# Turned weights in four buffers, half a projection between them, and a first gate and up that are scaled by 1/rms afterwards

## The chip, the cores and the metric

The kernel runs on one core of a Trainium2 chip. The metric is the device time of one execution in microseconds (us). Before the change it was 3081.7 us, the median of 3 runs (3077.83 to 3083.58). TensorE is called PE here, VectorE DVE, ScalarE ACT, GpSimd POOL and SyncE SP.

## The reference

Two layers run over two groups of tokens that share all weights: a sample of 512 tokens and a prompt of 1024. The model width is 1024, the hidden width of the channel mixer 2816.

```python
def fourier_mixer(x, g, w):
    b, s, d = x.shape
    h = rms_norm(x, g).astype(jnp.float32).reshape(b, s, N_FGROUPS, FGROUP_DIM)
    mixed = jnp.real(jnp.fft.fft2(h, axes=(1, 3), norm="ortho"))
    return mixed.reshape(b, s, d).astype(x.dtype) @ w

def swiglu_ffn(x, g, w_gate, w_up, w_down):
    h = rms_norm(x, g)
    return (jax.nn.silu(h @ w_gate) * (h @ w_up)) @ w_down

for i in range(DEPTH):          # DEPTH = 2
    x = x + (fourier_mixer(...) if i % 2 == 0 else attention_mixer(...))
    x = x + swiglu_ffn(x, norm_ffn[i], ffn_w_gate[i], ffn_w_up[i], ffn_w_down[i])
```

The change concerns layer 0 of the sample: the Fourier mixer with its projection by `w`, and the norm, gate and up of the channel mixer behind it. Since 1/rms is one number for each token, it can be multiplied in before the gate's product or behind it.

## The kernel before

**Blocks and precision.** The tokens are three blocks of 512: block 0 is the sample, blocks 1 and 2 are the prompt. Activations stand turned, 128 features on the partitions and 512 tokens along the row. Each operand of a product is kept as a high and a low half, and `mm3` (lines 247 to 249) makes three matmuls of it: high by high, high by low, low by high. `split` (240, 241) makes the halves: ACT copies the high one, DVE or, if asked, POOL subtracts for the low one. `weights` loads a 512 KB chunk on SP, ACT casts it (278) and POOL subtracts (279).

**Order.** A planner orders each engine's queue: an instruction may be put ahead of others that stand earlier in the program, when its inputs and buffers are ready by the planner's model. `pinned` forbids that for one instruction. On the chip each queue runs in the order so made. `tl` hands out tiles by tag; a tag has a fixed number of buffers (`BUFS`, line 150), and a new tile waits until the last use of the tile that held its buffer. `weave` (1122) advances a main generator and an auxiliary one by the numbers that they yield, so that the smaller share of its cost goes next. Tags that end in F are the main generator's, those in X the auxiliary one's.

**The sample's mixing.** The constants and rows are loaded, then `busy(56)` issues 56 dummy matmuls (258 to 262). `lead` (1173) weaves two things. `mixer` (428) squares and folds the rows (`prepared`, 396 to 412), scales and combines them (`unit`, 454), multiplies them along the tokens (`along`, 525) and handles the feature 64 of each group apart (`ends_folded`, 491; `stacked`, 607). `turned_weights` (613) builds the weights of the projection: `operand(n)` adds and subtracts the two halves of chunk n (631 on DVE, 632 on POOL), casts (634, ACT) and subtracts (635, POOL); `product(n)` multiplies it by the small Fourier matrix (9 matmuls), splits the result for the sample's own projection (`split` at 653) and writes a copy to memory (`cwd`) for the prompt. The operands `wm` have the four buffers of `acc` for the whole stage, with the sample's Fourier matrix and first combined rows in two of them. Two operands are made ahead of the first product. Raw chunks have two buffers (`rawX`), the sums `f` two (`rawF`).

**The sample's projection and first norm.** `follow` (1185) runs when all eight products are traced. `mixer_projection` (674) makes for each of 8 output chunks 25 matmuls, adds the residual on DVE (717 to 722), squares on ACT and adds up (333). The last chunk has `busy(10)` in it and `rstd_cols` (295) `busy(12)`. 1/rms is worked out by `rsqrt` (282) on DVE, spread over the partitions by `in_rows` (305), and `normed` (338) multiplies each chunk by it and splits it into the tile h, the low halves on POOL.

**The FFN of block 0** (`ffn`, 743) goes through 22 hidden chunks: gate and up, 24 matmuls each, silu on ACT (784), the product on DVE (785), the split into `mid`, and 8 down products of 3 matmuls, which run among the next chunk's gate and up and are added up on DVE (755). The first gate and up alternate. The gate's and up's results have one bank each (`gF`, two banks). Meanwhile the auxiliary generator `aux_0` (1198) loads the prompt's rows, mixes and projects them. Its first step, the loading, is taken before `follow`.

Of the kernel before, what the change touches and what calls it, by code (L numbers as in the profile page):

```python
# [17 lines left out]
P = 128  # L18
# [41 lines left out]
def dft_constants():  # L60
# [38 lines left out]
    for par in range(2):  # L99
        odd[64 * par + 1 : 64 * par + 64 : 2, [8 + 4 * par, 40 + 4 * par, 72 + 4 * par]] = 1.0  # L100
    alt = np.zeros((P, 4, 2, 64))
    for g in range(NC):
        alt[[g, 64 + g], g % 4, g // 4] = (-1.0) ** i
# [21 lines left out]
def trunk_kernel(ctx: ExitStack, tc: tile.TileContext, t: dict):  # L125
# [125 lines left out]
    early, resting = [], []  # L251
# [43 lines left out]
    def rstd_cols(y, sq, n):  # L295
# [4 lines left out]
        if first and not resting:  # L300
            resting.append(True)
            busy(12)
# [35 lines left out]
    def normed(b, gain, got, ab, held=None):  # L338
# [5 lines left out]
        if b in resident:  # L344
            for dc in range(NC):
                x = tmp()
                dve.scalar_tensor_tensor(x, resident[b][dc], gain[:, dc : dc + 1], r, op0=ALU.mult, op1=ALU.mult)
                split(h[:, 0, dc], h[:, 1, dc], x, eng=pool)
            got["h"] = h
            return  # L350
# [34 lines left out]
    def load_rows(seq):  # L385
# [6 lines left out]
        for c, x in enumerate(xs):  # L392
            (sp if c % 2 == 0 else act).dma_start(x, t[f"rows_{seq}"][:, c, :])
        whole[seq] = xs

    def prepared(seq, n, ga, gb, sums):
# [4 lines left out]
        for c, x in enumerate(whole[seq]):  # L401
# [8 lines left out]
            yield 1.0  # L410
# [17 lines left out]
    def mixer(seq, done, u, xrs, zz):  # L428
# [53 lines left out]
        def ends(c):  # L482

            return sums[c][:, 1].rearrange("p (j r a) -> p r j a", j=4, r=2)[:, :, :, 0]

        def groups(ap):
            return ap.rearrange("p (r j) -> p r j", r=2)

        z, zs = zz

        def ends_folded():
            for c in range(2):
                f = [col(8) for _ in range(2 * npair)]
                for i in range(npair):
                    ca, cb = 4 * i + c, 4 * i + 2 + c
                    dve.tensor_scalar(groups(f[2 * i]), ends(ca), r[:, ca : ca + 1], None, op0=ALU.mult)
                    if two:
                        dve.scalar_tensor_tensor(groups(f[2 * i + 1]), ends(cb), scal(cb)[0], groups(f[2 * i]), op0=ALU.mult, op1=ALU.add)
                for k in range(3):
                    at = slice(32 * k, 32 * k + 8)  # L500
                    if two:
                        dve.tensor_tensor(z[:, 2 * c, at], f[1], f[3], op=ALU.add)
                        dve.tensor_tensor(z[:, 2 * c + 1, at], f[1], f[3], op=ALU.subtract)
                    else:
                        dve.scalar_tensor_tensor(groups(z[:, c, at]), ends(c + 2), scal(c + 2)[0], groups(f[0]), op0=ALU.mult, op1=ALU.add)
# [854 lines left out]
```

## Time and profile before

| | |
|---|---|
| median of 3 runs | 3081.7 us (3077.83 to 3083.58) |
| the profiled execution | 3077.77 us, of which the span of instructions 3076.0 |
| PE busy in the span | 2985.8 us (97%) |
| DVE busy | 1642.7 us (53%) |
| ACT busy | 1219.5 us (40%) |
| POOL busy | 1279.8 us (42%) |
| mean granted clock of PE | 0.993 |

A row of a timeline has the start, the duration, the engine, the line, the operation, the tile written and those read, their shapes and how many such instructions are merged; in brackets the time that the engine stood idle before it, and what ended that. A row of groups has behind the count the busy time in us, the mean of one instruction in ns, and the idle time before them. A row of windows has the stretch and its length, then for each engine the busy time and the number of instructions, then the clock that PE was granted, as a share of the full one, the share of time in which the DMA engines were busy, and GB/s. PE's busy time counts dummy matmuls and those at a low clock in full, so a busy PE isn't always a useful one.

### The profile page before, as it was taken

To read this page: it belongs to the slowest core of one execution; us is meant where nothing else is said; L and a number is where in the kernel's file an instruction comes from. 1 tells how busy PE (TensorE), PEld (TensorE's weight loads), DVE (VectorE), ACT (ScalarE), POOL (GpSimd) and SP (SyncE) were. 2 spreads that over 40 slices of the span, in tenths; PEclk is the share of its full clock that TensorE was granted. 3 is DMA by queue.
4 is the path that set the end of the run, shared out by engine and by line. 5 is a ranking of instruction groups with operands and counts; after the bars stand their busy time and mean duration, and the time that the engine had idled before them with its cause. 6 is when DMAs were issued, how large, how long until landed. Compare 5 with 4: busy or idle time off the path is not lost.

```text
span 3076.0 us, 36978 instructions
## 1 busy us (share of the span) xinstructions
PE 2985.8 (97%) x14268; PEld 2448.0 (80%) x14268; DVE 1642.7 (53%) x2863; ACT 1219.5 (40%) x1749; POOL 1279.8 (42%) x583
## 2 busy tenths in 40 slices
PE   7999999999999999999999999999999999999999
PEld 5778888888877878888878788888787787877777
DVE  6775554634455543533464465665236555655556
ACT  4433332333466532333344577777324222222221
POOL 4434444443333454444433321222637644544452
PEclk8999999999999999999999999999999999999999
DMA  6435443332323544433343211212636411111111
GB/s 211 140 101 160 153 126 96 117 113 81 103 83 103 185 155 139 143 110 103 93 147 103 91 60 60 66 50 78 221 118 198 164 62 45 45 56 56 47 48 62
DMA packets 132080, 330.06 MB, mean 107 GB/s; under 512 B 14176, under 2 KB 28512, under 8 KB 131264
## 3 DMA queue, kind: packets, MB, share of 16 engines
q1 hardware_dynamic: 130112, 316.61, 32.0%
q0 software_dynamic: 928, 7.94, 0.7%
q10 hardware_dynamic: 864, 3.15, 0.3%
q8 instruction: 112, 1.84, 0.2%
q14 instruction: 64, 0.52, 0.1%
HBM read 280.45 MB, written 47.19 MB: 107 GB/s over the span
## 4 chain that ended last, share of the span: by engine, by line
PE 83%; POOL 5%; DVE 4%; DMA 3%; issue 3%; ACT 2%; SPq 0%; POOLq 0%; ACTq 0%; DVEq 0%
PE c L247 12%; PE c L248 12%; PE c L249 12%; PE g L249 10%; PE g L247 10%; PE g L248 10%; PE a L247 4%; PE a L249 4%; PE a L248 4%; PE c L1095 2%; POOL w L279 2%; POOL w L241 1%; DVE col L1078 1%; POOL h L241 1%; PE c L1028 1%
## 5 line engine op out<-in xcount | busy, mean ns | idle before, releaser
L279 POOL TENSOR_TENSOR w<-raw,w 128x1024 fp32r<-128x1024 f32 x354 | 846.1, 2400 | 1316.3 <-ACT w L278 1249.6
L755 DVE TENSOR_TENSOR acc<-c,acc 128x512 f32<-128x512 f32 x704 | 483.1, 689 | 473.5 <-PE c L249 469.8
L278 ACT CAST w<-raw 128x1024 fp32r<-128x1024 f32 x354 | 370.8, 1049 | 530.7 <-PE c L249 281.3
L247 PE MATMUL g<-h,w 128*128 128x512 f32 x1408 | 557.0, 396 | 4.8 <-ACT t L784 4.8
L248 PE MATMUL g<-h,w 128*128 128x512 f32 x1408 | 553.4, 393 | 0.6 <-POOL h L241 0.6
L249 PE MATMUL g<-h,w 128*128 128x512 f32 x1408 | 552.7, 393 | 0.0
L247 PE MATMUL c<-mid,w 128*128 128x512 f32 x1056 | 416.7, 397 | 11.6 <-DVE acc L755 9.1
L248 PE MATMUL c<-mid,w 128*128 128x512 f32 x1056 | 414.0, 392 | 2.2 <-DVE mid L241 2.2
L249 PE MATMUL c<-mid,w 128*128 128x512 f32 x1056 | 413.6, 392 | 0.0
L241 POOL TENSOR_TENSOR w<-raw,w 128x1024 fp32r<-128x1024 f32 (+1 forms) x101 | 228.3, 2268 | 337.5 <-ACT w L240 316.4
L865 DVE TENSOR_TENSOR acc<-c,acc 128x512 f32<-128x512 f32 x352 | 240.8, 689 | 191.3 <-PE c L249 190.6
L247 PEld LDWEIGHTS g<-h,w 128*128 128x128 f32 x1408 | 265.8, 189 | 59.5 <-ACT t L784 6.5
L249 PEld LDWEIGHTS g<-h,w 128*128 128x128 f32 x1408 | 266.0, 189 | 55.0 <-POOL w L279 0.3
L248 PEld LDWEIGHTS g<-h,w 128*128 128x128 f32 x1408 | 265.8, 189 | 53.4 <-POOL h L241 1.3
L247 PEld LDWEIGHTS c<-mid,w 128*128 128x128 f32 x1056 | 197.8, 188 | 73.7 <-DVE acc L755 20.3
L248 PEld LDWEIGHTS c<-mid,w 128*128 128x128 f32 x1056 | 198.5, 188 | 41.7 <-DVE mid L241 3.9
L249 PEld LDWEIGHTS c<-mid,w 128*128 128x128 f32 x1056 | 198.5, 188 | 40.5
L248 PE MATMUL c<-h,w 128*128 128x512 f32 x480 | 188.2, 392 | 3.2 <-POOL h L241 3.1
L247 PE MATMUL c<-h,w 128*128 128x512 f32 x480 | 189.1, 395 | 0.8 <-ACT h L240 0.8
L249 PE MATMUL c<-h,w 128*128 128x512 f32 x480 | 187.0, 390 | 0.0
L240 ACT CAST w<-raw 128x1024 fp32r<-128x1024 f32 (+1 forms) x101 | 100.3, 1000 | 202.6 <-PE a L249 86.6
L1077 DVE TENSOR_REDUCE col<-a 128x1 f32<-128x1024 f32 (+1 forms) x96 | 100.4, 1046 | 128.2 <-PE a L249 128.0
(349 smaller groups left out, 4775.6 us busy)
## 6 DMA issues: line engine op xcount, KB each, us to landing
raw<-in_down_dram SPq DMA_DIRECT2D x110, 512.0 KB, 3.6
raw<-in_gate_dram SPq DMA_DIRECT2D x88, 512.0 KB, 3.6
raw<-in_up_dram SPq DMA_DIRECT2D x88, 512.0 KB, 3.7
raw<-in_qkv_dram SPq DMA_DIRECT2D x36, 512.0 KB, 3.9
t<-xres SPq DMA_DIRECT2D x56, 256.0 KB, 3.9
raw<-in_wo_dram SPq DMA_DIRECT2D x24, 512.0 KB, 3.9
raw<-in_gate_dram SPq DMA_DIRECT2D x44, 256.0 KB, 2.7
raw<-in_up_dram SPq DMA_DIRECT2D x44, 256.0 KB, 3.1
```

What stands on the lines that cost most here:

```text
L240: act.copy(hi, src)
L241: eng.tensor_tensor(lo, src, hi.bitcast(F32), op=ALU.subtract)
L247: pe.matmul(out, lh, rh, start=first, stop=False)
L248: pe.matmul(out, lh, rl, start=False, stop=False)
L249: pe.matmul(out, ll, rh, start=False, stop=last)
L278: pinned(act.copy(flat[:, 0], raw)) if early else act.copy(flat[:, 0], raw)
L279: pool.tensor_tensor(flat[:, 1], raw, flat[:, 0].bitcast(F32), op=ALU.subtract)
L755: dve.tensor_tensor(acc[dc], ps, acc[dc], op=ALU.add)
L865: dve.tensor_tensor(acc, ps, acc, op=ALU.add)
L1028: pe.matmul(c[:, i : i + 1], sq[:, i * P : (i + 1) * P], ones[:, 0:1], start=True, stop=True)
L1077: dve.tensor_reduce(st[:, 0:1], s_in, op=ALU.max, axis=AX.X)
L1095: pe.transpose(tr[:, i * P : (i + 1) * P], p[:, kc * P : (kc + 1) * P], ident)
```

## The change

- `busy(56)` becomes `busy(36)`; the 10 and the 12 dummy matmuls around the projection's end go.
- The operands `wm` get four buffers of their own in the slot hB; the sample's mixed rows and constants move to hA. Three operands are made ahead of the first product. In the mixer the second pair of units comes ahead of the multiplications along the tokens, and more is yielded, so that products stand at other places.
- Four products are traced within `lead`, and the other four one by one between the first four steps of the projection.
- The table for feature 64 (`stage`) takes a buffer of `rawF` and is loaded behind the first two chunks. The groups of features have another order, so that the small reads and writes of `ends_folded` have fewer instructions; the first multiplication of each goes to ACT.
- Each projection step splits its residual times the gain straight into h, the low halves on DVE. `normed` isn't called for block 0. 1/rms is copied into `first["r"]`, and `ffn` multiplies gate and up of block 0 by it, for all 22 hidden chunks.
- The prompt's rows are loaded later, all on SP, within the weave of the FFN of block 0, which runs 10 steps alone first.

```diff
-        if first and not resting:
-            resting.append(True)
-            busy(12)
...
-            (sp if c % 2 == 0 else act).dma_start(x, t[f"rows_{seq}"][:, c, :])
+            (act if seq == "s" and c % 2 else sp).dma_start(x, t[f"rows_{seq}"][:, c, :])
...
-            yield 1.0
+            yield 4.0
...
-                    dve.tensor_scalar(groups(f[2 * i]), ends(ca), r[:, ca : ca + 1], None, op0=ALU.mult)
+                    act.activation(f[2 * i], ends(ca), AF.Copy, scale=r[:, ca : ca + 1])
...
-            yield 1.0
+            yield 5.0
         r64 = mpt.tile([P, 516], F32R, tag="r64", name=f"r64_{seq}")
         second = []
+        for c in range(2):
+            second.append(unit(1, c))
+            yield 5.0
         if two:
             ends_folded()
-            for c in range(2):
-                second.append(unit(1, c))
-                yield 1.0
...
-            if j < 2 and not two:
-                second.append(unit(1, j))
...
-            w = acc_tile("wm", [2, 2, TB], F32R)
+            w = moving_w[n % 4]
...
-        operand(0)
-        yield
-        operand(1)
-        yield
+        for n in range(3):
+            operand(n)
+            yield
         for n in range(NC):
             product(n)
-            if n + 2 < NC:
-                operand(n + 2)
+            if n + 3 < NC:
+                operand(n + 3)
             yield
...
             resident[0] = accumulators()
+            first["h"] = h_tile("B")
...
-                if not two and n == NC - 1:
-                    busy(10)
...
+                if not two:
+                    split(first["h"][:, 0, n], first["h"][:, 1, n], x, gain=g_ffn[0][:, n : n + 1])
                 new_residual(b, n, x, stays=not two)
...
+            if here:
+                dve.tensor_tensor(ga, ga, first["r"], op=ALU.mult)
+                dve.tensor_tensor(up, up, first["r"], op=ALU.mult)
             act.activation(s, ga, AF.Silu)
...
-    stage = h_slot("stage", F32, "A")[:, 0:D]
-    sp.dma_start(stage[0:96], t["wf64"])
+    stage = tl("raw", [D], F32, "rawF")
+    slot_a = h_slot("wm", F32R, "B")[:, 0 : 16 * TB].rearrange("p (s h k n) -> p s h k n", s=4, h=2, k=2)
+    moving_w = [slot_a[:, i] for i in range(4)]
...
-    busy(56)
+    busy(36)
...
         next(ws)
-        stacked(w64[0:96], stage[0:96], 64)
+        sp.dma_start(stage[0:96], t["wf64"])
         m = mixer("s", got_s, u_s, xrs_s, zz_s)
         for k, v in enumerate(m):
             yield v
-            if k in (1, 3) or k >= 5:
-                next(ws, None)
+            if k == 4:
+                stacked(w64[0:96], stage[0:96], 64)
+            if k in (1, 3, 6) or k in (8, 10, 12, 14):
+                next(ws)
+
+    def follow():
+        m = mixer_projection("s", got_s)
+        for k in range(4):
+            next(m)
+            next(ws)
+            yield 1.0
         for _ in ws:
             yield 1.0
-
-    def follow():
-        yield from mixer_projection("s", got_s)
+        yield from m
         next(early[2])
         early.clear()
-        yield from normed(0, g_ffn[0], first, "B")
+        first["r"] = tl("ss", [TB], F32, "ssF")
+        act.copy(first["r"], in_rows(rstd[0]))
...
     weave(lead(), 1.0)
-    cur[0] = "X"
-    for _ in range(1):
-        next(x_0)
     weave(follow(), 1.0)
-    weave(ffn(0, 0, lambda: first["h"]), FFN_US, x_0, (45.0 + 60.0) * SLACK)
+    weave(ffn(0, 0, lambda: first["h"]), FFN_US, x_0, (80.0 + 60.0) * SLACK, 10)
```

More of the change, by code (lines that the diff above doesn't have):

```diff
@@ L249, in mm3 @@
         pe.matmul(out, ll, rh, start=False, stop=last)
-    early, resting = [], []
+    early = []
     nxt, first = {}, {}
@@ L651, in product @@
                     for b in range(2):
-                        pe.matmul(od[0:96], odd[:, 8 - j : 104 - j], w[:, b, 0], start=j == 0 and b == 0, stop=j == 3 and b == 1)
+                        pe.matmul(od[0:96], odd[:, 8 - 2 * j : 104 - 2 * j], w[:, b, 0], start=j == 0 and b == 0, stop=j == 3 and b == 1)
                 split(wt[:, 0, k], wt[:, 1, k], ps)
@@ L699, in mixer_projection @@
             for i, b in enumerate(blocks):
-                if (i if two else n % 2) == 0:
+                if two and i:
+                    e, o = sides()
+                elif not two and n > 3 and n % 2:
+                    e, o = (tl("c", [TB], F32, "cX", pools["psX"]) for _ in range(2))
+                else:
                     e, o = bank(), bank()
-                else:
-                    e, o = sides()
                 c0 = 258 * i
```

46 lines of the change are left out of this document (19 added, 27 removed).

## Prediction

> **What bounds the kernel now.** I read the page's busy rows first, then a table of windows cut at the stages of the sample block, then the timeline of those stages.
>
> ```profile
> span 3076.0 us, 36978 instructions
> ...
> PE   7999999999999999999999999999999999999999
> ```
>
> TensorE (PE) is busy 97% of the span. Only the first of 40 slices, 77 us each, is below nine tenths. Whatever this change wins by keeping PE fed it can win only there and in the thin places just behind.
>
> ```profile
> core 0: us, PE busy (x) PEld busy (x) DVE busy (x) ACT busy (x) POOL busy (x), PEclk, DMA share, GB/s
> 22.70:84.30 61.60, 41.21 (x145) 28.41 (x143) 42.68 (x81) 30.15 (x55) 27.89 (x16) 0.78 0.60 197
> 84.30:108.40 24.10, 24.10 (x201) 23.98 (x200) 16.59 (x47) 7.86 (x14) 3.77 (x4) 1.00 0.40 141
> 108.40:118.90 10.50, 9.59 (x78) 9.01 (x77) 5.14 (x20) 6.24 (x14) 6.71 (x4) 1.00 0.50 157
> 118.90:131.10 12.20, 11.53 (x48) 8.75 (x48) 9.86 (x16) 10.56 (x20) 10.08 (x8) 1.00 0.10 39
> 131.10:141.90 10.80, 7.36 (x24) 5.57 (x24) 10.80 (x19) 6.19 (x10) 4.76 (x2) 0.84 0.39 123
> 160.00:280.00 120.00, 111.19 (x589) 92.19 (x588) 77.53 (x163) 45.99 (x75) 48.79 (x21) 0.99 0.39 126
> 280.00:540.00 260.00, 260.00 (x1276) 220.27 (x1275) 133.22 (x249) 75.20 (x97) 112.36 (x47) 1.00 0.41 128
> ```
>
> The columns are busy times and instruction counts. From 22.7 to 84.3 the weights are turned and the sample is mixed. From 84.3 to 108.4 comes its projection, 201 matmuls in 24.1 us, 0.12 us each: dense, at clock 1.00. From 108.4 to 118.9 lies the normalization, then the first gate and up (48 matmuls) to 131.1, and the change to the second gate. From 280 on PE has no idle time, with DVE busy 133 of 260 us.
>
> ```profile
> 483.94 0.39 PE L247 MATMUL c<-mid,w 128*128 128x512 f32 x1
> ...
> 484.62 0.39 PE L247 MATMUL g<-h,w 128*128 128x512 f32 x1
> ```
>
> Three 512-wide matmuls in a stream take 0.68 us, 0.227 each. So the 48 of the first gate and up need 10.9 us of their 12.2, and the 24 records behind them 5.4 of 10.8 us.
>
> In 22.7 to 84.3 the code issues eight products of 9 matmuls (72 x 0.227 = 16.3 us) and 69 mixing matmuls of 0.12 (8.3): 24.6 us of work in 61.6. The other 37 us are waits and a clock of 0.78. Who makes PE wait there?
>
> ```profile
> L635 POOL TENSOR_TENSOR wm<-f,wm 128x1024 fp32r<-128x1024 f32 x8 | 18.9, 2369 | 24.1 <-ACT wm L634 24.1
> ...
> L632 POOL TENSOR_TENSOR f<-raw 128x512 f32<-128x512 f32 x8 | 11.3, 1413 | 19.6 <-DMA raw<-in_wf_dram 19.4
> ...
> L241 DVE TENSOR_TENSOR w<-g,w 128x512 fp32r<-128x512 f32 x16 | 10.9, 687 | 10.7 <-ACT w L240 10.7
> ...
> L631 DVE TENSOR_TENSOR f<-raw 128x512 f32<-128x512 f32 x8 | 8.0, 1006 | 0.0
> ```
>
> One operand costs POOL 1.41 + 2.37 = 3.8 us, eight 30 us. POOL is busy 27.9 of the 61.6 us, so it isn't full either; POOL itself stands still 24.1 us for ACT's cast and 19.6 for a load.
>
> ```profile
> 31.19 1.26 POOL L632 TENSOR_TENSOR f<-raw 128x512 f32<-128x512 f32 x1 [6.20 <-DMA raw<-in_wf_dram]
> ...
> 58.29 2.37 POOL L635 TENSOR_TENSOR wm<-f,wm 128x1024 fp32r<-128x1024 f32 x1 [5.38 <-ACT wm L634]
> ```
>
> At 31.19 it had waited 6.2 us for the third weight chunk, at 58.29 5.4 us for a cast. This is a ring: two operand buffers, so POOL waits for ACT, ACT for a product to evacuate, PE for POOL. DVE is the fullest engine with 42.7 of 61.6 (69%).
>
> **The change part by part.** Sums are against the profiled execution, 3077.8 us as timed (span 3076.0 and 1.8 around it); the median of the runs shown, 3081.7, is 3.9 above.
>
> *Normalization of the first h.* The rows of the gap are these.
>
> ```profile
> 109.34 2.50 PE L262 MATMUL g<-ones 128*128 128x128 f32 x20 [0.84 <-DVE acc L718]
> ...
> 112.49 2.92 PE L262 MATMUL g<-ones 128*128 128x128 f32 x24
> ...
> 133.81 0.60 PE L247 MATMUL g<-h,w 128*128 128x512 f32 x1 [2.74 <-ACT t L784]
> ```
>
> The h tile no longer waits for 1/rms. Each projection step now issues an ACT cast and a DVE subtraction, and the gate can follow the last projection matmul at once. Of 78 dummy matmuls 42 go: the 10 and 12 here (44 records, each matmul being two), and 20 at the start. What remains on PE of the 10.5 us for this block are 8 records for the sums of squares and 8 for the diagonal products, at the dummies' 2.50/20 = 0.125 each: 2.0 us. Term: **-8.5** (0 if something else as long takes the place). The first gate and up had 1.3 us of waits for POOL's lower halves: **-1.3**. The last h chunk is late by one residual update, a cast and a subtraction, about 3 us, and is read 42 matmuls (9.5 us) into the gate: hidden. If it weren't, 3 us.
>
> 1/rms is now needed only when the first gate and up end. Its chain fitted inside 10.5 us with the dummies in it, and the 48 matmuls give it 10.9: it is ready, just. What is late next is the second gate, at 133.81: it waited 2.74 us for the silu that frees its bank, 1.28 of it a table load, and the clock fell behind that (0.84 in the row of 131.1 to 141.9).
>
> ```profile
> 131.86 1.28 ACT L784 ACT_TABLE_LOAD   x1
> ```
>
> The multiplication by 1/rms comes in front of that silu: **+0.6**.
>
> *22 gate and up pairs are multiplied, not one.* The branch holds for all of the block, so DVE gets 44 instructions. Their price is that of the existing product of the same shape and place:
>
> ```profile
> 480.12 0.70 DVE L785 TENSOR_TENSOR g<-g,t 128x512 f32<-128x512 f32 x1 [1.41 <-PE g L249]
> 481.67 0.69 DVE L241 TENSOR_TENSOR mid<-g,mid 128x512 fp32r<-128x512 f32 x1 [0.85 <-ACT mid L240]
> ...
> 486.18 0.69 DVE L755 TENSOR_TENSOR acc<-c,acc 128x512 f32<-128x512 f32 x1 [0.67 <-PE c L249]
> ```
> ```profile
> 486.86 0.60 ACT L784 ACTIVATE t<-g 128x512 f32<-128x512 f32 x1 [5.22 <-PE g L249]
> ```
>
> Read 480.12 as the end of one up: DVE multiplies (0.70), ACT casts, DVE subtracts until 482.36. By the row of 483.94 above, the first down matmul that reads it starts at 483.94, so there are 1.6 us to spare against 0.7 more. The gate's multiplication sits ahead of the silu of 486.86, which here ends 9 us before the next gate wants the bank (72 matmuls on from 480.1, at 496.4). DVE has 0.67 us idle between accumulations (486.18), nearly the 0.70 needed. So 44 x 0.69 = 30 us of DVE work lie in a stage where PE has no idle time and DVE is half empty. Queued behind a multiplication on DVE are the accumulations, for which PE's two down banks wait; a slip of 0.7 us is less than the 1.36 us (six matmuls) between two accumulations. I take **0** from 280 on. From above the bound is all 30 us exposed; below zero nothing, it only adds.
>
> *Prompt rows later.* Row loads move from before the projection to behind the sample's last use of their slot, all on SP, and their 32 DVE passes (x 0.69: 22 us) move from the gap into the FFN, spread by larger yields. In 160 to 280 PE lost 8.8 us while DVE was crowded. Spreading should save some of it, the 44 multiplications give some back, and the loads (4 MB) now share SP's queue with the FFN weights. Bounds -8.8 to +8.8; I take **-1**, near nothing, as both sides act on the same row.
>
> *Four buffers, three ahead, and half a projection between.* Products 4 to 7 leave the mixing stage, and their PE, POOL and DVE work lies beside projection steps 0 to 3. That takes 4 x 9 x 0.227 = 8 us of PE work out of the serial part, and from DVE per product one addition, two subtractions and a copy: 1.0 + 2 x 0.69 + 0.7 = 3.1, so 12 us. The third load no longer shares the DMA with 4 MB of prompt rows. The row-64 table is loaded behind the first two chunks and copied later, so ACT no longer stands before it with the row sums behind:
>
> ```profile
> 14.80 1.05 ACT L609 CAST eo<-stage 96x1024 fp32r<-96x1024 f32 x1 [5.98 <-DMA stage<-in_wf_dram]
> ```
>
> That lets about 3 of the DVE's microseconds start before 22.7. Small group reads go to ACT:
>
> ```profile
> 40.85 2.48 DVE L496 TENSOR_SCALAR col<-x,r_s 128x8 f32<-128x8 f32 x2
> 40.89 2.40 POOL L635 TENSOR_TENSOR wm<-f,wm 128x1024 fp32r<-128x1024 f32 x1 [4.79 <-ACT wm L634]
> ```
>
> A 128x8 operation took 1.2 us each while POOL held 40.89 to 43.29; it cannot do so on ACT. The Trainium skill, SBUF — State Buffer, Who interferes with whom, says that DVE in a two-port mode, or with two SBUF inputs, is shut out until the POOL instruction ends. The trace agrees: 40.85 + 2.48 ends with POOL at 43.3.
>
> Sum: DVE's 42.7 us less 12 for the products, 2.5 for those reads and those 3 is about 25; the best it can be is that with DVE full, the worst today's 69%: 25 to 36 us instead of 61.6. Starting at 22.7, the mixing ends at 48 to 59. Four steps of product and projection cost PE 2.0 + 3.0 and DVE 3.1 + 2.1 (its 16.6 of the projection's row, over 8), so 5.2 us each: 21 us. Then four projection steps of 3.0, and up to 3 us for the h chunks of steps 0 to 3, which must wait for the operand buffers in the same slot: 12 to 15. End 81 to 95, against 108.4. The upper end rests on a rate that this stage shows today, so I take 95: **-13**. Below stand PE's own work, 24.6 + 24.1 from 22.7, so 71 (-37); above, no gain (0), if the ring only moves.
>
> Sum: -8.5 - 1.3 + 0.6 + 0 - 1 - 13 = -23.2; 3077.8 - 23.2 = 3054.6, rounded to 3055.
>
> *Fewer dummies* price nothing by themselves where PE has real work behind them. At the start stand 56 now:
>
> ```profile
> 9.46 13.49 PE L262 MATMUL g<-ones 128*128 128x128 f32 x112
> ```
>
> 36 end 4.8 us earlier (20/56 of 13.49), and PE may begin cold; today it runs at 0.78 there in spite of them. The Trainium skill, TensorE: Matmul & The Clock Gate, Part 1, says that an idle window of about 3.4 us halves the clock. In this trace 2.74 us did. It speaks against removing them, and is rival 2.
>
> **The rivals.**
>
> 1. *Slower: the gate's multiplication queues behind the last accumulation.* In program order it stands there. Then each next gate waits not 0 but today's wait of 133.81, 2.74, less the table load's 1.28, plus 0.7: 2.16 us, at 21 boundaries, 45 us; with the slow clock behind it more. Above 23.2/21 = 1.1 us a boundary the change loses. For: that one boundary did wait. Against: the silu of 486.86 also stands behind them in program order and runs early. 3055 + 45 = 3100. Chance 0.08.
>
> 2. *The ring only moves.* Raw weights keep two buffers, so the third operand ahead is still as late as its load, and PE goes cold between products. Then the term of -13 is lost: 3068. Chance 0.14. That the change doesn't do what it says belongs here: four buffers, but never more than two full.
>
> 3. *DVE is shut out by POOL.* The lower halves of h move from POOL to DVE, with two SBUF inputs, as the additions of L631 have (1.0 us against 0.69).
>
> ```profile
> L347 DVE SCALAR_TENSOR_TENSOR t<-acc,gains,c 128x512 f32<-128x512 f32 x8 | 5.8, 745 | 4.6 <-POOL h L241 2.3 <-PE c L311 2.3
> ```
>
> Eight at 0.75 us, each lengthened as at 40.85, by up to a POOL instruction of 2.4, cost up to 8 x 1.65 = 13 us more at the projection's end; I take three quarters, 10: 3065. Chance 0.06. By the Trainium skill, in the section of SBUF — State Buffer named above, it is just what to expect; the rule there speaks against this part of the change.
>
> 4. *It all overlaps.* POOL's 30 us stay ahead of PE; the projection ends near 78, close to the 71 of PE's own work, -30 instead of -13, and I keep the rest: 3038. Chance 0.12.
>
> **How the numbers follow.** The forecast, 3055, has 0.60; its own range is 3045 to 3063. Faster and slower are counted from 0.2% of 3081.7, 6.2 us, about what a measurement of this kernel can tell from no change: under 3075.5 and over 3087.9. The forecast, rivals 3 and 4 and most of rival 2 are faster: 0.60 + 0.06 + 0.12 + 0.10 = 0.88; the rest of rival 2 within, 0.04; rival 1 slower, 0.08. The range goes from 3036, just under rival 4, to 3076, rival 2 with the crowded row at its upper bound, and leaves rival 1 and the tails out.
>
> **What would show it.** PE: no row of L262 behind the projection, the first gate right at its last matmul. The projection's end near 95 us. Silu's release of the second gate about 3.4 us late. Windows of the FFN behind 280 full, with about 10% more DVE. POOL's wait for ACT's cast well under 24 us. I am wrong if PE shows a wait for the silu at each of the 21 boundaries, if the mixing stage is still 60 us long, or if h's subtractions take 2 us each.

## The result, and the profile after

The changed kernel takes **3048.0 us**, the median of 4 runs (3045.96 to 3048.51), against 3079.8 (3077.25 to 3083.58) of the kernel before in the same comparison: a ratio of 0.9895, with a 95% interval of 0.9877 to 0.9912. That is 32 us less. The prediction was 3055 in a range of 3036 to 3076. The profiled execution has a span of 3045.8 us where the kernel before had 3076.0, 30.2 less.

The page of the changed kernel, its span and PE's busy share in 40 slices:

```profile
span 3045.8 us, 36762 instructions
...
PE   7999999999999999999999999999999999999999
```

As before, only the first slice is thin. The table of windows of the changed kernel, cut at its own stages (busy time and instructions of PE, PE's weight loads, DVE, ACT and POOL, then PE's clock, DMA share, GB/s):

```profile
18.58:59.70 41.12, 29.63 (x122) 20.94 (x120) 34.52 (x64) 25.28 (x48) 25.06 (x15) 0.79 0.64 202
59.70:92.27 32.57, 30.70 (x224) 28.59 (x224) 27.43 (x61) 16.64 (x31) 7.11 (x6) 1.00 0.44 129
92.27:108.89 16.62, 14.09 (x72) 11.35 (x70) 7.71 (x22) 9.71 (x16) 10.61 (x5) 1.00 0.74 248
108.89:144.84 35.95, 34.27 (x155) 28.14 (x155) 27.95 (x45) 16.10 (x27) 15.00 (x8) 1.00 0.43 150
160.00:280.00 120.00, 115.37 (x577) 95.42 (x576) 84.27 (x164) 49.23 (x83) 53.40 (x22) 0.99 0.36 116
280.00:540.00 260.00, 258.41 (x1301) 219.84 (x1300) 150.79 (x291) 77.48 (x99) 109.74 (x46) 1.00 0.43 137
```

Set them against the windows of before. Turning and mixing ended at 84.3 and now end at 59.7. The projection ended at 108.4; now it ends at 92.3, with four products inside. The stage of 10.5 us behind it is gone, its dummies of L262 with it. In 160 to 280 PE still has 4.6 us without work (it had 8.8). In 280 to 540 it lost nothing before and now has 1.6 us of idle time, with DVE at 151 us instead of 133 (13% more); in the repeat of the changed kernel below (c_after) it has 0.6.

The costliest groups of the turning of the weights (busy time, mean ns of one, idle time before them and what ended it), and the group of the lower halves of h, from two windows of the changed kernel:

```profile
L623 POOL TENSOR_TENSOR wm<-f,wm 128x1024 fp32r<-128x1024 f32 x8 | 19.1, 2387 | 16.4 <-ACT wm L622 16.2
...
L241 DVE TENSOR_TENSOR w<-g,w 128x512 fp32r<-128x512 f32 x16 | 10.7, 684 | 2.9 <-ACT w L240 2.9
```

```profile
L244 DVE SCALAR_TENSOR_TENSOR h<-acc,gains,h 128x512 fp32r<-128x512 f32 x8 | 6.7, 865 | 1.0 <-ACT h L243 1.0
```

POOL's wait for ACT's cast fell from 24.1 to 16.4 us, and DVE's wait for ACT's copy of the turned weights from 10.7 to 2.9. An h subtraction on DVE takes 0.87 us, not the 2 of rival 3.

The timeline around the first gate of the changed kernel (start, duration, engine, line, operation; in brackets the idle time before it):

```profile
92.27 0.39 PE L247 MATMUL g<-h,w 128*128 128x512 f32 x1
...
105.88 1.05 ACT L278 CAST w<-raw 128x1024 fp32r<-128x1024 f32 x1 [0.84 <-PE g L249]
...
105.91 0.70 DVE L775 TENSOR_TENSOR g<-g,ss 128x512 f32<-128x512 f32 x1 [3.85 <-PE g L249]
...
106.95 1.28 ACT L777 ACT_TABLE_LOAD   x1
...
108.89 0.50 PE L247 MATMUL g<-h,w 128*128 128x512 f32 x1 [1.73 <-ACT t L777]
```

The gate follows the projection at once (92.27; its third matmul then waits 0.80 us for POOL's lower half of a weight), and 1/rms is there when the gate is done: DVE multiplies at 105.91. The second gate then waits for silu, 1.73 us, because the table load of 1.28 starts only at 106.95, behind the multiplication, which ends at 106.61, and behind a weight cast on ACT, which ends at 106.93. So much looks like the prediction. The experiments show that much of the gain comes from elsewhere than it said.

### The profile page after: what moved, and what is told of

Same layout as the page of the kernel before. It is cut to its first block, busy times and chain, and to the rows that moved or that the text cites. A ratio compares the mean times of both kernels' runs of the same rounds, so it can differ in the third digit from the quotient of the medians.

```text
span 3045.8 us, 36762 instructions
## 1 busy us (share of the span) xinstructions
PE 2968.1 (97%) x14184; PEld 2434.7 (80%) x14184; DVE 1666.7 (55%) x2883; ACT 1224.3 (40%) x1758; POOL 1271.5 (42%) x575
## 4 chain that ended last, share of the span: by engine, by line
PE 82%; POOL 3%; DVE 3%; DMA 3%; issue 2%; ACT 1%; SPq 0%; POOLq 0%; ACTq 0%; DVEq 0%
PE c L247 12%; PE c L248 12%; PE c L249 12%; PE g L249 10%; PE g L247 10%; PE g L248 10%; PE a L247 5%; PE a L249 4%; PE a L248 4%; PE c L1088 2%; POOL w L279 1%; DVE col L1071 1%; POOL w L241 1%; PE c L1021 1%; POOL h L241 0%
## 5 line engine op out<-in xcount | busy, mean ns | idle before, releaser
L247 PEld LDWEIGHTS c<-mid,w 128*128 128x128 f32 x1056 | 197.9, 188 | 74.3 <-DVE acc L745 18.3
```

Source lines behind the costliest of these rows:

```text
L247: pe.matmul(out, lh, rh, start=first, stop=False)
```

## The experiments

All twelve kernels below were timed beside the kernel before, in four comparisons: c_after to e3; e4, v_renorm, b1 and e10; e12, e11 and v_pool; e5. The kernel before had 3082.0, 3080.0, 3079.2 and 3080.8 us in them, so medians from different comparisons can differ by 1 to 3 us for that alone, and the ratios are the safer figure. The table has the median, the ratio to the kernel before with its 95% interval, and five places read from PE's timeline of the profiled execution: the start of the first product of the turned weights, the end of the mixing (its last matmul; products of the turned weights may follow), the end of the projection, the start of the first gate, the start of the first down product; all in us.

| kernel | median | ratio, interval | first product | mixing ends | projection ends | first gate | first down |
|---|---|---|---|---|---|---|---|
| before | 3079 to 3082 | 1 | 22.7 | 84.4 | 108.5 | 118.9 | 147.3 |
| c_after (changed) | 3047.8 | 0.9890, 0.9876 to 0.9905 | 18.7 | 59.8 | 92.5 | 92.4 | 115.2 |
| e1_norm_back | 3043.0 | 0.9874, 0.9859 to 0.9889 | 18.4 | 59.3 | 90.7 | 101.6 | 119.4 |
| e2_no_interleave | 3048.2 | 0.9894, 0.9877 to 0.9910 | 19.5 | 59.1 | 91.7 | 91.5 | 116.5 |
| e3_two_buffers | 3047.5 | 0.9885, 0.9870 to 0.9900 | 19.2 | 57.2 | 90.8 | 90.7 | 114.0 |
| e4_no_mult | 3042.5 | 0.9880, 0.9866 to 0.9893 | 18.7 | 59.9 | 92.7 | 92.5 | 115.7 |
| v_renorm | 3053.3 | 0.9912, 0.9898 to 0.9925 | 19.3 | 58.9 | 92.3 | 92.2 | 111.6 |
| b1_rows_late | 3060.4 | 0.9936, 0.9923 to 0.9950 | 22.8 | 77.5 | 101.7 | 112.0 | 134.7 |
| e10_old_order | 3059.5 | 0.9936, 0.9923 to 0.9948 | 18.3 | 77.4 | 105.6 | 105.7 | 128.8 |
| e12_order_only | 3051.4 | 0.9908, 0.9892 to 0.9925 | 18.1 | 61.4 | 96.4 | 96.3 | 119.5 |
| e11_old_mixer_order | 3048.0 | 0.9895, 0.9881 to 0.9910 | 18.4 | 57.5 | 93.0 | 92.8 | 116.7 |
| v_pool | 3046.5 | 0.9892, 0.9877 to 0.9907 | 18.5 | 59.5 | 92.2 | 92.1 | 116.4 |
| e5_busy56 | 3049.2 | 0.9895, 0.9878 to 0.9913 | 23.4 | 61.0 | 93.8 | 93.6 | 115.8 |

An interval is some 10 us wide. A difference of under 4 us between two of these kernels is therefore read from the places in the timeline, not from the medians.

### Undoing one part at a time

The theory to begin with was the prediction's: first norm about -9, buffers and half projection -13.

**c_after** is the changed kernel, unaltered.

> The changed kernel again, unaltered, as the yardstick of the three others on the same chip. Both theories: 3048 us, ratio to the kernel before 0.9895, within 0.15%.

**e1_norm_back** undoes the first norm's part (the 10 and the 12 dummies come back with it, in lines left out here).

```diff
+        if b in resident:
+            for dc in range(NC):
+                x = tmp()
+                dve.scalar_tensor_tensor(x, resident[b][dc], gain[:, dc : dc + 1], r, op0=ALU.mult, op1=ALU.mult)
+                split(h[:, 0, dc], h[:, 1, dc], x, eng=pool)
...
-                if not two:
-                    split(first["h"][:, 0, n], first["h"][:, 1, n], x, gain=g_ffn[0][:, n : n + 1])
...
-            if here:
-                dve.tensor_tensor(ga, ga, first["r"], op=ALU.mult)
-                dve.tensor_tensor(up, up, first["r"], op=ALU.mult)
...
+        yield from normed(0, g_ffn[0], first, "B")
```

> Block 0 is normalized ahead of the first gate again, with its 22 dummies, and no gate or up is multiplied by 1/rms; all else as changed. Theory (the sum's terms -8.5, -1.3 and +0.6 are right): +9 us against the changed kernel, 3057; the projection still ends near 92 us and the first gate starts 10 us behind it. Rival (the gap only moved to the second gate and to later waits): +3 us or less, 3051. Second rival (the 44 multiplications cost something after all): 0 or faster.

**e2_no_interleave** and **e3_two_buffers** undo the half projection between, and the buffers.

```diff
-        for k in range(4):
-            next(m)
-            next(ws)
-            yield 1.0
         for _ in ws:
             yield 1.0
```
```diff
-        for n in range(3):
+        for n in range(2):
             operand(n)
...
-            w = moving_w[n % 4]
+            w = moving_w[n % 2]
...
-            if n + 3 < NC:
-                operand(n + 3)
+            if n + 2 < NC:
+                operand(n + 2)
```

> All eight products are traced ahead of the projection, four buffers and three ahead kept. Theory (the interleaving carries most of the 16 us by which the projection ends earlier): PE's and DVE's work of four products, four times 2.0 us of PE and 3.1 us of DVE, goes back ahead of the projection, +8 to +12 us, 3056 to 3060, the projection's end at 100 to 104 us. Rival (buffers and order carry it, PE is fed as well without): +2 or less, the projection's end under 95.

> Two operand buffers and two operands ahead, as before; the half projection between the products stays. Theory (four buffers and three ahead break the ring of waits): the ring returns in the mixing stage, POOL waits over 20 us for ACT's cast instead of 16.4, +5 to +9 us, 3053 to 3057. Rival (the raw loads set the pace, since POOL still waits 13.3 us for them, and only the order of work counts): within 2 us, 3046 to 3050.

All three theories fell, and in each case a rival written down with it came. Undoing the half projection cost nothing (3048.2; the projection ends at 91.7). Undoing the buffers cost nothing either (3047.5; 90.8). Undoing the first norm's part made the kernel **faster**, 3043.0 (3042.54 to 3044.51) against 3047.8 (3046.51 to 3051.2): no run of the one is as slow as the fastest of the other.

The timeline of e1_norm_back behind the projection shows the old gap back in full:

```profile
90.53 2.39 PE L262 MATMUL g<-ones 128*128 128x128 f32 x20
...
93.88 2.92 PE L262 MATMUL g<-ones 128*128 128x128 f32 x24
...
101.59 0.73 PE L247 MATMUL g<-h,w 128*128 128x512 f32 x2
```

From 90.53 to 101.59 stand the 44 records of the 22 dummies and the matmuls of the norm. Where does it win that back? I took from DVE's timeline the start of the product of up and silu for each hidden chunk of block 0, and subtracted that of the changed kernel. e1 is 5.5 us late at chunk 0, 1.5 at chunk 3, then 2.3 early at chunk 5, 4.7 at chunk 8, 4.0 at chunk 21. So it loses 5.5 us in front and wins about 10 between the chunks 0 and 8, in which the prompt's rows are squared, folded and mixed. What it does there without is the multiplications.

### The multiplications by 1/rms

**e4_no_mult** leaves them out from hidden chunk 1 on, **v_renorm** replaces them by a second scaling of h (beside the edit of e4), **v_pool** moves half of them to POOL.

```diff
-            if here:
+            if here and fc == 0:
                 dve.tensor_tensor(ga, ga, first["r"], op=ALU.mult)
                 dve.tensor_tensor(up, up, first["r"], op=ALU.mult)
```

> The changed kernel without the multiplications by 1/rms for hidden chunks 1 to 21 of block 0 (42 of the 44 are left out, so these chunks aren't scaled). Theory formed from the run with the normalization put back, which lost 5.5 us ahead of the first product of gate and up and won 10 us between hidden chunks 0 and 9: the multiplications cost about 10 us in the stage where the prompt's passes crowd DVE, and nothing behind 400 us; 3038. Rival (the prediction's step, they are hidden everywhere): 3046 to 3049.

```diff
+            if here and fc == 0:
+                for dc in range(NC):
+                    x = tmp()
+                    dve.scalar_tensor_tensor(x, acc[dc], g_ffn[0][:, dc : dc + 1], first["r"], op0=ALU.mult, op1=ALU.mult)
+                    split(h[:, 0, dc], h[:, 1, dc], x, eng=pool if dc % 2 else dve)
```

> The multiplications by 1/rms stay for hidden chunk 0 alone; then h is scaled in its own tile (8 products of the residual, the gain and 1/rms on DVE, 8 casts on ACT, the lower halves on DVE and POOL in turn) ahead of the second gate. If the 42 multiplications cost 10 us: 3038 plus 1 to 3 us in which the second gate waits for its chunks, 3039 to 3041, faster than both kernels and than the one with the normalization put back. If they cost nothing: 3048 to 3051.

```diff
-                dve.tensor_tensor(up, up, first["r"], op=ALU.mult)
+                if fc == 0:
+                    dve.tensor_tensor(up, up, first["r"], op=ALU.mult)
             act.activation(s, ga, AF.Silu)
+            if here and fc:
+                pool.tensor_tensor(s, s, first["r"], op=ALU.mult)
```

> For hidden chunks 1 to 21 of block 0 the silu's result is multiplied by 1/rms on POOL instead of up's product on DVE: 21 DVE instructions fewer, 21 of about 1.4 us more on POOL. If the 8 us that the multiplications cost come from DVE's queue in the crowded stage: about half comes back, 3043 to 3046. If POOL's instructions shut DVE out or come late ahead of the product: 3048 or more.

e4 takes 3042.5 us, where 3038 was expected: 5.3 less than c_after, some 3 by the two ratios, and 4.7 by the two spans. By the same count it is 0.6 us late at chunk 0, then early by 2.2 at chunk 3, 5.9 at chunk 5, 8.4 at chunk 8 and 8.0 at chunk 21. Behind chunk 8, that is from 276 us on, the multiplications cost nothing; ahead of it 8 us. (At the end of the span 4.7 us of it are left. In this execution of e4 5 us go at one place far behind the multiplications: at 2320.28 PE waits 2.92 us for DVE's accumulation, and its matmuls take 0.63 us for the next 5 us. Whether e4 always loses them there isn't shown.)

The window in which most of it is lost, of c_after and then of e4:

```profile
180.00:230.00 50.00, 45.54 (x199) 35.98 (x198) 43.05 (x67) 20.18 (x31) 17.74 (x8) 0.97 0.34 106
```

```profile
180.00:230.00 50.00, 49.14 (x235) 40.01 (x234) 36.83 (x65) 22.04 (x36) 18.01 (x8) 1.00 0.35 105
```

DVE is busy 43 of 50 us with the multiplications and 37 without, and PE has 45.5 us of work against 49.1. The timeline of c_after at the worst boundary shows how an up's multiplication gets late:

```profile
198.69 2.03 DVE L459 TENSOR_SCALAR t<-x_p,r_p 1x512 f32<-1x512 f32 x1
...
200.64 0.68 DVE L776 TENSOR_TENSOR g<-g,ss 128x512 f32<-128x512 f32 x1
...
201.38 0.68 DVE L778 TENSOR_TENSOR g<-g,t 128x512 f32<-128x512 f32 x1
...
202.09 0.58 ACT L240 CAST mid<-g 128x512 fp32r<-128x512 f32 x1 [2.37 <-DVE g L778]
...
202.73 0.60 PE L247 MATMUL c<-mid,w 128*128 128x512 f32 x1 [2.10 <-ACT mid L240]
...
203.45 0.79 PE L248 MATMUL c<-mid,w 128*128 128x512 f32 x1
```

DVE stands in one small operation of the prompt from 198.69 to 200.72. In e4 the same operation (L459) takes 0.47 us. POOL's row of c_after, then DVE's and POOL's of e4:

```profile
195.68 4.76 POOL L279 TENSOR_TENSOR w<-raw,w 128x1024 fp32r<-128x1024 f32 x2 [5.03 <-ACT w L278]
```

```profile
193.79 0.47 DVE L459 TENSOR_SCALAR t<-x_p,r_p 1x512 f32<-1x512 f32 x1
193.84 5.05 POOL L279 TENSOR_TENSOR w<-raw,w 128x1024 fp32r<-128x1024 f32 x2 [3.74 <-ACT w L278]
```

POOL subtracts the lower halves of two weights in both. In c_after the operation starts while POOL is at it, and ends 0.28 us behind POOL's end (200.44); in e4 it starts just ahead of POOL. So the loss at this boundary is more than the multiplications' own 0.69 us each: with them a small operation has come to lie beside POOL. The multiplication (L776) comes behind it, then the product with silu (L778), then ACT's cast, and PE has waited 2.10 us for `mid`. The two matmuls behind the wait take 0.60 and 0.79 us instead of 0.39: the clock went down too. At another boundary it is the gate's multiplication:

```profile
143.14 0.69 DVE L775 TENSOR_TENSOR g<-g,ss 128x512 f32<-128x512 f32 x1
...
144.02 1.04 ACT L278 CAST w<-raw 128x1024 fp32r<-128x1024 f32 x1 [1.03 <-PE g L249]
144.97 0.59 ACT L777 ACTIVATE t<-g 128x512 f32<-128x512 f32 x1
...
145.61 0.50 PE L247 MATMUL g<-h,w 128*128 128x512 f32 x1 [1.68 <-ACT t L777]
```

It starts at 143.14, when the prompt's passes let it; ACT has meanwhile begun a weight cast (144.02), silu follows at 144.97, and the next gate has waited 1.68 us. This is the mechanism of rival 1, at 1.68 us instead of its 2.16, but, besides the second gate's wait of 1.73, at this one of the 21 boundaries only.

v_renorm did not give what I expected: 3053.3. Its first down product comes 3.6 us earlier than c_after's, but chunk 1 is 6.6 us late:

```profile
107.45 2.34 POOL L279 TENSOR_TENSOR w<-raw,w 128x1024 fp32r<-128x1024 f32 x1 [1.98 <-ACT w L278]
107.58 2.76 DVE L784 SCALAR_TENSOR_TENSOR t<-acc,gains,ss 128x512 f32<-128x512 f32 x1
...
110.58 2.37 POOL L279 TENSOR_TENSOR w<-raw,w 128x1024 fp32r<-128x1024 f32 x1 [0.79 <-ACT w L278]
110.86 3.30 DVE L784 SCALAR_TENSOR_TENSOR t<-acc,gains,ss 128x512 f32<-128x512 f32 x2
...
114.08 0.68 DVE L241 TENSOR_TENSOR mid<-g,mid 128x512 fp32r<-128x512 f32 x1
...
114.82 0.79 PE L248 MATMUL c<-mid,w 128*128 128x512 f32 x1 [2.12 <-DVE mid L241]
```

DVE's scaling has two SBUF inputs, the residual and 1/rms. While POOL subtracts a weight's lower half (107.45 to 109.79), one such instruction takes 2.76 us, and two take 3.30, against 0.69 for the multiplications that read PSUM. The subtraction for `mid` at 114.08 is then late and PE waits 2.12 us. The Trainium skill, SBUF — State Buffer, Who interferes with whom, has this rule (the prediction tells it), and here it sets the delay of chunk 1; at the lower halves of h, where the prediction weighed it as rival 3, it did not decide. By chunk 8 the delay is down to 0.1 us, and the profiled execution, 3049.4, is the fastest of the four. So what makes the other three 3053 isn't shown. v_pool is early by 2.3 us at chunk 21, a quarter of e4's gain, which the medians can't tell from nothing (3046.5 against 3047.8).

### What shortens the mixing

As neither buffers nor half projection were missed, two kernels asked what else it is. **b1_rows_late** is the kernel before with the late loading of the prompt's rows alone.

```diff
-    slot = h_slot("eo", F32R, "B")
+    slot = h_slot("eo", F32R, "A")
...
-    stage = h_slot("stage", F32, "A")[:, 0:D]
+    stage = h_slot("stage", F32, "B")[:, 0:D]
...
-    cur[0] = "X"
-    for _ in range(1):
-        next(x_0)
...
-    weave(ffn(0, 0, lambda: first["h"]), FFN_US, x_0, (45.0 + 60.0) * SLACK)
+    weave(ffn(0, 0, lambda: first["h"]), FFN_US, x_0, (80.0 + 60.0) * SLACK, 10)
```

The larger yields of the change (4.0 for each row, 5.0 for each unit) are in it too.

> The kernel before with one part of the change: the prompt's rows are loaded after the sample's projection (the sample's mixed rows take the other slot, as in the change) and the weave of the FFN of block 0 has the change's numbers. Theory (what was mis-sized is the load: the third weight chunk queues behind 4 MB of rows, and the PE idle of 7.3 us at 27.5 goes): projection's end at 99 to 102 instead of 108.4, in all -7 to -12, 3070. Rival (the ring of two buffers sets the pace anyway): projection's end at 106 or later, 3075 or more.

It takes 3060.4 us: **-15 to -24 us** by its interval, -14.8 by the two spans, more than the theory had, from one part that the prediction had at -1. There are two places. First, the load of the third weight chunk (L620): its issue, and in the row with KB its time from issue to landing, in us. The kernel before, and then b1:

```profile
17.13 2.41 SPq L393 DMA_DIRECT2D x_p<-in_rows_p_dram  x3
21.47 0.33 SPq L620 DMA_DIRECT2D raw<-in_wf_dram  x1
...
raw<-in_wf_dram SPq DMA_DIRECT2D x1, 512.0 KB, 9.6
```

```profile
21.69 0.33 SPq L620 DMA_DIRECT2D raw<-in_wf_dram  x1
...
raw<-in_wf_dram SPq DMA_DIRECT2D x1, 512.0 KB, 3.5
...
25.38 1.28 POOL L632 TENSOR_TENSOR f<-raw 128x512 f32<-128x512 f32 x1 [0.18 <-DMA raw<-in_wf_dram]
```

The chunk is issued at almost the same time in both, when DVE's addition (L631) has freed its buffer, so the order in SP's queue did not delay the issue. What differs is the transfer: before, six prompt rows, issued on SP and ACT between 17.13 and 19.11, were still on their way at 21.47, and the chunk landed behind them, 9.6 us after its issue instead of 3.5. POOL starts on it at 25.38 instead of 31.19. The projection ends at 101.7 instead of 108.5, 6.8 us earlier. The ring, though, is as it was:

```profile
L635 POOL TENSOR_TENSOR wm<-f,wm 128x1024 fp32r<-128x1024 f32 x8 | 19.0, 2374 | 25.5 <-ACT wm L634 25.5
```

POOL waits 25.5 us for ACT's cast, where it waited 24.1. Second, the stretch from the first gate to the first down product, of before and then of b1, and b1's projection:

```profile
118.90:147.25 28.35, 24.23 (x95) 18.74 (x96) 23.44 (x39) 18.14 (x30) 17.24 (x11) 0.94 0.28 96
```

```profile
77.50:101.70 24.20, 24.18 (x201) 23.97 (x200) 17.05 (x47) 7.66 (x13) 4.94 (x6) 1.00 0.58 194
...
111.90:134.65 22.75, 19.68 (x76) 15.63 (x77) 6.26 (x10) 11.73 (x21) 15.55 (x11) 0.85 0.30 111
```

The prompt's passes ran in this stretch: DVE was busy 23.4 of 28.4 us, and is busy 6.3 of 22.8 without them. The stretch got 5.6 us shorter. The projection keeps its 24.2 us. The remaining 2 us of the span's 14.8 come later.

**e10_old_order** is the counterpart: the changed kernel with everything undone that orders the turning and mixing.

```diff
-        for c in range(2):
-            second.append(unit(1, c))
-            yield 5.0
...
+            if j < 2 and not two:
+                second.append(unit(1, j))
...
-            if k in (1, 3, 6) or k in (8, 10, 12, 14):
-                next(ws)
+            if k in (1, 3) or k >= 5:
+                next(ws, None)
```

It also has the edits of e2 and e3.

> The changed kernel with two operand buffers, two operands ahead, no half projection between, and the mixer's old order (second units among the multiplications along the tokens, a product at each step): what stays of the change ahead of the projection is the late rows, the small reads on ACT with fewer instructions, the row-64 table's place and the 36 dummies. Theory (these carry the gain): the projection's end at 91 to 95, 3045 to 3050. Rival (buffers, half projection and order each replace the other, and together carry it): the projection's end at 100 or later, 3055 or more.

The rival was right: 3059.5, the projection's end at 105.6, 13 us late. Order, buffers and half projection together carry it, though two of them were worth nothing when undone alone. Late rows, small reads on ACT, the place of the row-64 table and fewer dummies leave the mixing ending at 77.4, no earlier than b1's 77.5, though its first product starts 4.5 us earlier. So no gain of these last three is seen at the mixing's end, as long as the ring is there. (Its projection takes 4 us longer than b1's; 3.4 of them are one wait for DVE's residual at 88.8.)

**e12_order_only** (the edits of e2 and e3 together) and **e11_old_mixer_order** (the first two hunks of e10, and products at the steps 7, 9, 11 and 13) split it.

> The changed kernel with two operand buffers, two operands ahead and no half projection between: of what the run with the old order undid, only the mixer's new order stays (second units ahead of the multiplications along the tokens, a product at every second step). Theory (the order alone carries the 13 us that the run with the old order gave back): the projection's end at 90 to 94 us, 3045 to 3050. Rival (buffers ahead and the half projection can each replace the other, so that only both undone show): the end at 100 or later, 3055 or more.

> The counterpart: four buffers, three ahead and the half projection stay, and the mixer's order is the old one (second units among the multiplications along the tokens, products two steps apart from there). Theory (order alone): the projection's end at 100 or later, 3055 or more. Rival (buffers and half projection): 90 to 95, 3045 to 3050.

With the new order alone the projection ends at 96.4, 4 us late; with buffers and half projection alone at 93.0, 0.5 late; with neither, 13 late. Each can replace most of the other. The groups of POOL's second instruction show it, in e10 and then in e12:

```profile
L625 POOL TENSOR_TENSOR wm<-f,wm 128x1024 fp32r<-128x1024 f32 x8 | 18.9, 2366 | 26.5 <-ACT wm L624 26.5
```

```profile
L623 POOL TENSOR_TENSOR wm<-f,wm 128x1024 fp32r<-128x1024 f32 x8 | 19.0, 2379 | 16.3 <-ACT wm L622 16.3
```

Two operand buffers serve as well as four once a product comes only at every second step: POOL's wait for ACT is 16.3 us with two buffers and the new order, and 16.4 with four. Between e12 and the changed kernel the windows show another clock; that it accounts for all of the 4 us isn't shown. Windows of 4 us, of c_after, then of e12, then of e10:

```profile
44.00:48.00 4.00, 4.00 (x20) 3.14 (x19) 3.20 (x5) 3.71 (x7) 3.60 (x3) 0.76 0.52 155
48.00:52.00 4.00, 3.44 (x22) 2.78 (x21) 3.68 (x5) 1.43 (x4) 3.29 (x3) 1.00 1.00 369
```

```profile
44.00:48.00 4.00, 4.00 (x16) 3.35 (x16) 3.59 (x6) 2.73 (x5) 0.00 (x0) 0.50 0.30 82
48.00:52.00 4.00, 4.00 (x15) 3.37 (x15) 1.51 (x3) 1.35 (x3) 2.98 (x3) 0.50 0.79 252
52.00:56.00 4.00, 4.00 (x17) 3.38 (x16) 3.18 (x6) 2.46 (x5) 2.22 (x2) 0.59 1.01 309
```

```profile
56.00:60.00 4.00, 3.36 (x12) 2.65 (x11) 2.98 (x5) 2.38 (x4) 0.24 (x2) 0.64 0.99 292
```

In e12 PE has work in all of 44 to 56 and runs at 0.50 to 0.59; in c_after it is back at 1.00 by 48. In e10 PE is in part without work (3.36 of 4 us) and at 0.64 behind 56, where e12 is at 1.00.

### The dummies at the start

**e5_busy56** has `busy(56)` for `busy(36)`.

> The changed kernel with the 56 dummies at the start instead of 36. Theory (the sum's price of nothing): the first product starts about 4 us later, near 22.7, but what sets the pace behind it is DVE and the loads, so the projection ends within 2 us of 92.5 and the time is 3046 to 3050. Rival (the dummies held PE back): +4 us, 3052. Second rival (fewer dummies let the clock fall): a clock well above 0.73 between 18 and 40 us and a projection that ends at 90 or earlier, 3045 or less.

The first product starts 4.7 us later, at 23.4, the projection ends 1.3 later, the product of up and silu in chunk 8 comes 0.6 later, and the median is 3049.2 (3042.71 to 3052.51): no difference that can be told. The price of nothing holds. In the first rival's direction 1 us may be left. The second rival has its clock (0.84 in 18 to 40 instead of 0.75 by the windows, and behind the dummies, in 24 to 40, 0.77 instead of 0.65) but not its gain.

Not tried: early prompt rows in the changed kernel (the sample's mixed rows hold their slot), and the small reads on DVE again. Nor was one more edit of the change undone alone: the odd steps of the sample's projection behind the third take their two result banks from another pool.

## Why the prediction was right, and where it wasn't

The time was right by luck: two errors of opposite sign cancelled for the most part. The first norm's part was forecast at -9.2 us and cost about 4.5, an error of some 14. The rest was forecast at -14 and brought about -35 (spans of 3076.0 and 3041.4), an error of some 21. The difference, 7, is what the time is under the forecast. By the prediction's own terms:

- **First h, -8.5 - 1.3 + 0.6 = -9.2.** Mechanism right, size too large. From the projection's end to the start of the first product of up and silu the changed kernel needs 7.3 us less than e1; but its projection, with eight casts and subtractions in it, also ends 1.8 us later (0.5 of it stands already at the mixing's end), so 5.5 us reach chunk 0. The term argued that the last chunk's cast and subtraction are hidden and gave the others no price. Of the 1.3 us that it calls waits for POOL's lower halves, PE's timeline of before has one wait, of 0.64.
- **Second gate late, forecast at 3.4 us.** It waited 1.73, less than the 2.74 of before. In e1, without the multiplication and with the prompt's passes gone from there, it waited 1.34, near the table load's 1.28. So the multiplication, together with the weight cast on ACT beside it, adds 0.4 to the wait here. In the kernel before, ACT squared a prompt row until 131.85, right ahead of the table load: that was the rest of the old wait.
- **The 44 multiplications, 0.** Right from 280 us on, as the prediction bounded it. Wrong ahead of that: 8 us, between hidden chunks 0 and 8. The step that failed is the one that put "the 44 multiplications give some back" into the same -1 as the spread rows. The price of 0 was read from a row at 480 us, where DVE is half empty, and carried no price for the stage in which DVE is 74% busy without them (e4 in 180 to 230) and 86% with them. With this the first norm's part as a whole costs about 4.5 us instead of gaining 9. Nor is it shown that it would gain without the multiplications: e4 is 4.0 us ahead of e1 at chunk 21, but the two end within 0.5 us of each other by medians and by spans.
- **Prompt rows later, -1 (bounds -8.8 to +8.8).** The largest error: -15 to -24 when done alone, outside its bounds. Two amounts were left out. The prompt's passes lengthened the stretch from the first gate to the first down product by 5.6 us; the windows of 118.9 to 141.9 quoted in the prediction show DVE 81% and 100% busy there, and the sum took nothing for it. And the third weight chunk's delay, which the prediction names, was booked under the next term.
- **Buffers, three ahead, half projection, -13 for the projection's end.** It came to -16: 6.8 of them are the rows', by b1, and the remaining 9 the order's, the buffers' or the half projection's. The step "this is a ring: two operand buffers" failed in part: two buffers do nearly as well when a product comes at every second step and the second units stand ahead. That reordering was in the diff, and the prediction gave it no term. The estimate of DVE's time (25 to 36 us for 61.6) was near: the window from 18.6 to 59.7 is 41 us.
- **Fewer dummies, nothing.** Right.

Of the rivals, the first's mechanism appeared at one of the 21 boundaries beside the second gate's, and a like one for the up at another. The second (the ring only moves) is what e10 does, without the reordering; the changed kernel isn't there. The third was wrong at 0.87 us for an h subtraction. The fourth did not come: the projection ends at 92, not 78.

Single reversals don't add up here. In profiled spans, the kernel before has 3076.0; late rows alone 3061.2; all but order, buffers and half projection 3058.4; all 3045.8; all but the first norm's part 3041.4. A chain tells more of what a part is worth than single reversals do, but in another order the shares may differ.

**Best version.** e1_norm_back, the change without its first norm's part, is faster than both kernels: 3043.0 us, a ratio of 0.9874 (0.9859 to 0.9889).

## What to carry to other kernels

Price an added instruction in the fullest stage it runs in, not in a typical one: the same multiplication cost nothing behind 280 us and 8 us in all ahead of that. A load hoisted early delays the transfers issued behind it (9.6 us instead of 3.5 for one chunk here, though its issue was not late), and the work that it releases then lands in the next thin place, so price the load, the transfers that it meets and its consumers in one term. And before crediting a change's parts, undo them in pairs: two remedies for the same wait hide each other when each is undone alone.

## What the runs showed of the hardware

The granted clock stayed at 0.50 in e12 through 44 to 52, and was still 0.59 in 52 to 56, though PE was busy in all of these windows with matmuls of 256 to 512 columns (6 of the 39 in 44 to 55.5 had a single row); in c_after it was 0.76 in 44 to 48 and then 1.00. The Trainium skill, TensorE: Matmul & The Clock Gate, Part 1, has the full clock back after about 3.4 us of sustained work. That held in e2 behind the second gate's wait, in PE's timeline,

```profile
109.56 0.79 PE L247 MATMUL g<-h,w 128*128 128x512 f32 x1 [2.72 <-ACT t L777]
...
112.71 0.39 PE L248 MATMUL g<-h,w 128*128 128x512 f32 x1
```

where the clock falls behind 2.72 us of idle time and is back 3.2 us later; the wait of 1.73 us at the same place in the changed kernel left it at 0.40 us a matmul, while its wait of 2.10 us at 202.73 lowered it, as shown above. In e12's mixing some 11 us of work without a gap, from 44 on, did not bring it back. What differs there isn't settled.
